# Even mixer of a two-layer hybrid network: latent products in two stream items, output projection from an earlier head, three transpose banks, float32 dilated groups

## The chip, the cores and the metric

One core of a Trainium2 chip runs the whole network in one launch. The metric is the device time of that launch in microseconds (us). Before the change the median of three runs is 1437.24 us (1437.18 to 1438.7).

## The reference, cut to what matters

512 tokens with 1024 features go through two layers; each adds a mixer and a gated feed-forward network (FFN) to the residual x. The change is almost wholly in the mixer of layer 0:

```python
def even_mixer(h, positions, w_in, q_norm, w_uq, kv_norm, w_ukv, w_out):
    proj = h @ w_in
    ...
    for gi, (window, dilation) in enumerate(DSW_GROUPS):      # (128,1), (512,4), (2048,16)
        og, lg = dilated_window_attention(q[:, :, sl], k[:, :, sl], v[:, :, sl], window, dilation)
    ...
    y_a = jnp.sum(wts[..., None] * jnp.stack(outs, axis=0), axis=0)   # 4 heads
    qm = (rmsnorm(c_q, q_norm) @ w_uq)                                # 12 latent heads
    kv = (rmsnorm(c_kv, kv_norm) @ w_ukv)
    ...
    y_b = causal_softmax_attention(q_full, k_full, v_m, (MLA_NOPE + MLA_ROPE) ** -0.5)
    return jnp.concatenate([y_a, y_b], axis=-1) @ w_out
```

The other mixer (a state-space scan, SSD, and stick-breaking attention), both FFNs and the norms are computed as before.

## The kernel before, in words

Activations lie with features on the 128 partitions and tokens along the free axis, so a tile is 128 x 512. Every large product keeps float32 accuracy by splitting both operands into a rounded part and a rest (hi and lo, type float32r) and doing three products: hi·hi, lo·hi, hi·lo (`mm3`, L113 is the one line that issues them). A weight chunk is loaded (`wraw`, SP queue), ACT copies it to `whi` (L220), and DVE, or POOL in the FFNs, subtracts to give `wlo` (L222). There are two buffers of each.

PE works strictly in the order in which the program was written (`InOrder`); the other engines' orders are set by a scheduler that replays the dependences. The even mixer is written as two interleaved sequences:

- A loop over 16 heads: twelve latent (MLA) heads in six pairs, and 2 x 2 dilated heads (each treats the three dilation groups g = 0, 1, 2 of one head). For each head: its scores (bank tag `s`), softmax (L580 to L584 on DVE and ACT), transposes of the probabilities (tag `t`), the copy to `pth`/`ptl` (hi on ACT, lo on DVE; L601/L602 in latent heads, L954/L955 in dilated ones), the products with the values (tag `o`), and `head_out` (L618 on ACT, L619 on DVE), which adds the two 64-partition halves of `o` into `yp`. The next head's scores stand between this head's value products.
- A `Stream` of items that fill PE between those steps, piece by piece (three products of 512 columns each, `st.fill`): the projections for the dilated heads (`d{p}{g}{s}`, tag `proj`), the latent products (`m{pr}`), the splitting of y (`y`) and the output projection (`o{m}`). `st.until(name)` drains the stream up to an item; `st.held` keeps an item back until a given head. `_load` fetches the chunk of the current item and of the one after it.

An item `m{pr}` (`run_mla`) does, all in `proj` banks: the value product (evicted by `vt`, L761), the key product (`knp`, L766), and two query products (`rt`, L775, split L265/L266); after the first of those the values are transposed and split (`token_split`, L629/L630). PSUM has eight banks of 512 columns: in this phase `proj`, `s`, `t` and `o` have two each. The output projection multiplies seven of the eight tiles of y in items `o0` to `o7`, released at head 14; the eighth tile (the second dilated pair's) follows in `run_tail`, eight outputs alternating between `s` and `proj`. `residual` (L367, DVE) adds each to x. Then `ffn` begins: its first two weight chunks, `norm` (`xh` on ACT, `xl` on DVE, L331/L332), the sum of squares.

In SSD, after the scores of 16 heads, `gate_norm(0)` (L1433) forms a row of 1/rms values by PE into a `t` bank, copied by ACT (`rsr`, L311); it stood at head 14, just ahead of two `gate` transposes, which use `t` as well.

Of the kernel before, what the change touches and what calls it, by code (L numbers as in the profile page):

```python
# [52 lines left out]
F_M, F_D0, F_D1 = (1, 1, 2), (2, 1.5, 3), (2, 2, 4)  # L53
# [65 lines left out]
class Stream:  # L119
# [12 lines left out]
    def _load(self, i):  # L132
        if i < len(self.items) and i not in self.loaded:
            self.loaded[i] = self.items[i][1]()

    def step(self, upto=None):

        while True:
            if self.gen is None:
# [3 lines left out]
                self._load(self.at + 1)  # L143
# [41 lines left out]
class Builder:  # L185
# [169 lines left out]
    def run_tail(self, src, kt, y, banks=("proj",)):  # L355

        def run(w):
            for m in range(KT):
                ps = self.psum(banks[m % len(banks)])
                self.gemm(ps, w, m * P, P, 0, {kt: y[kt][0]}, {kt: y[kt][1]}, [kt])  # L360
                self.residual(m, ps)
                yield

        return f"t{kt}", lambda: self.wchunk(src, D), run

# [4 lines left out]
    def build(self):  # L370
# [29 lines left out]
        with self.phase("l0", s=2, t=2, o=2) as pool:  # L400
            self.even_mixer(pool)
# [219 lines left out]
    def token_split(self, pool, src, tag, bufs):  # L621
# [5 lines left out]
        pv = pt.rearrange("p (b h d) -> p b h d", b=NB, h=2)  # L627
        v = pool.tile([P, NB, 2, 2, 64], F32R, tag=tag, name=self.nm(tag), bufs=bufs)
# [16 lines left out]
    def even_mixer(self, pool):  # L645
# [109 lines left out]

        def run_mla(pr):
            def run(w):
                vps = self.psum("proj")
                self.gemm(vps, w, 640, P, 0, klh, kll, [0])
                vt = pool.tile([P, T], F32, tag="tmp", name=self.nm("vt"), bufs=TMP)  # L760
                nc.vector.tensor_tensor(vt, vps, kr, op=ALU.mult)  # L761
                yield
                kps = self.psum("proj")
                self.gemm(kps, w, 512, P, 0, klh, kll, [0])
                knp = pool.tile([P, T], F32, tag="knp", name=self.nm("knp"), bufs=1)
                nc.vector.tensor_tensor(knp, kps, kr, op=ALU.mult)  # L766
                yield
                qs = []
                for e in range(2):
                    qps = self.psum("proj")  # L770
                    for i in range(2):
                        self.gemm(qps, w, e * P + i * 256, P, 256, qlh, qll, [i], i == 0, i == 1)
                        yield
                    t = pool.tile([P, T], F32, tag="tmp", name=self.nm("rt"), bufs=TMP)
                    nc.vector.tensor_tensor(t, qps, qt[e], op=ALU.mult)  # L775
                    qs.append(self.split(t, pool, **QK))
                    if e == 0:
                        v = self.token_split(pool, vt, "v", 3)
                yp = pool.tile([P, T], F32, tag="yp", name=self.nm("yp"), bufs=6)
                mla[pr] = qs, v, yp, knp  # L780

            return f"m{pr}", lambda: self.wchunk(a["wm0"][pr], 768), run

        def run_out(m):
            def run(w):
                yh, yl = {k: y[k][0] for k in range(7)}, {k: y[k][1] for k in range(7)}
                for ps in self.proj_pieces(w, yh, yl, range(7)):
# [3 lines left out]
            return f"o{m}", lambda: self.wchunk(a["wo0"][m], 896), run  # L791

        def run_y():
            def run(w):
                for i in range(6):
# [7 lines left out]
        def y_split(kt, yp):  # L803
# [7 lines left out]
               for p in range(2)]  # L811
        m = [run_mla(pr) for pr in range(6)]
        st = Stream(dsw[0][:3] + m[:1] + dsw[0][3:4] + m[1:2] + dsw[0][4:6] + m[2:3] + dsw[0][6:]
                    + dsw[1][:2] + m[3:4] + dsw[1][2:4] + m[4:5] + dsw[1][4:6] + m[5:] + dsw[1][6:]
# [921 lines left out]
```

## Time and profile before

| | |
|---|---|
| runs, median of three | 1437.24 us |
| profiled execution, own time | 1438.86 us |
| its span, first to last instruction | 1437.1 us |
| busy: PE, DVE, ACT, POOL | 96%, 59%, 47%, 32% |
| chain that ended last: PE, DVE, ACT, DMA | 80%, 11%, 5%, 1% |

The even mixer fills the first 340 us or so, its FFN follows to about 700, then SSD and stick-breaking attention to about 1020, the output projection of that mixer and the second FFN. A busy PE is not a PE at its peak: a product of 512 columns is shown as about 0.4 us long, but the next one starts 0.23 us later. So lost time must be looked for as idle time before instructions and as a lower granted clock (PEclk, 1.00 is full), not as a share of busy time.

### The profile page before, as it was taken

Reading aid. Unit: us, or ns where it says so; the run is one execution under the profiler, and the core shown is the slowest. Engines: PE = TensorE matmul, PEld = TensorE weight load, DVE = VectorE, ACT = ScalarE, POOL = GpSimd, SP = SyncE. Lnnn points to the kernel's source line nnn. Section 1 sums busy time; section 2 is a strip of 40 time slices with the busy share of each in tenths; the row PEclk is TensorE's granted clock in tenths of the full one; section 3 lists DMA queues with packets and bytes.
Section 4 is the critical chain, followed back from the end, with each engine's and each line's share of the span. In section 5 each row is a group of like instructions: output and inputs, shape, how many; then the busy total and the mean of one; then the engine's idle time right before and its main releaser. Section 6 shows DMA issues by size and latency. Waiting matters only on the chain.

```text
span 1437.1 us, 17873 instructions
## 1 busy us (share of the span) xinstructions
PE 1383.2 (96%) x6788; PEld 1141.8 (79%) x6788; DVE 845.6 (59%) x1313; ACT 681.7 (47%) x1119; POOL 454.7 (32%) x297
## 2 busy tenths in 40 slices
PE   7898989899999999999999998999999999999997
PEld 5687777787888888888878887787888888888886
DVE  7978678756555555221478775889555555552124
ACT  5478658744433333222355555787344333332222
POOL 2100000002655555444302620222025555554441
PEclk9999999999999999999999999999999999999999
DMA  4322112122232332333222111111233232333333
GB/s 166 112 70 63 56 55 72 40 67 88 88 103 88 103 94 97 94 94 98 88 88 89 59 60 46 59 45 48 77 96 96 95 103 89 102 99 90 101 95 99
DMA packets 40261, 121.19 MB, mean 84 GB/s; under 512 B 5232, under 2 KB 8304, under 8 KB 40176
## 3 DMA queue, kind: packets, MB, share of 16 engines
q1 hardware_dynamic: 38160, 117.92, 26.3%
q10 hardware_dynamic: 2016, 2.14, 0.5%
q8 instruction: 53, 0.87, 0.3%
q14 instruction: 32, 0.26, 0.1%
HBM read 114.80 MB, written 2.10 MB: 81 GB/s over the span
## 4 chain that ended last, share of the span: by engine, by line
PE 80%; DVE 11%; ACT 5%; issue 3%; DMA 1%; POOL 0%; SPq 0%; DVEq 0%; ACTq 0%; POOLq 0%
PE proj L113 50%; PE o L113 19%; PE z L113 5%; PE s L113 2%; PE t L116 2%; PE t L113 2%; DVE wlo L222 2%; DVE cv L1153 1%; ACT whi L220 1%; ACT s L582 1%; DVE xl L332 0%; DVE ptl L602 0%; ACT s L584 0%; DMA x<-in_x 0%; DVE x L367 0%
## 5 line engine op out<-in xcount | busy, mean ns | idle before, releaser
L222 POOL TENSOR_TENSOR wlo<-wraw,whi 128x1024 fp32r<-128x1024 f32 (+1 forms) x135 | 315.2, 2336 | 579.4 <-ACT whi L220 576.1
L220 ACT ACTIVATE whi<-wraw 128x1024 fp32r<-128x1024 f32 (+3 forms) x219 | 222.0, 1015 | 362.0 <-PE proj L113 324.7
L113 PE MATMUL proj<-xh,whi 128*128 128x512 f32 x844 | 343.6, 407 | 8.7 <-ACT xh L331 6.6
L113 PE MATMUL proj<-xh,wlo 128*128 128x512 f32 x844 | 334.2, 396 | 1.3 <-DVE wlo L388 1.1
L113 PE MATMUL proj<-xl,whi 128*128 128x512 f32 x844 | 334.3, 396 | 0.7 <-DVE xl L332 0.7
L113 PE MATMUL proj<-act,whi 128*128 128x512 f32 (+1 forms) x748 | 219.3, 377 | 0.0
L113 PEld LDWEIGHTS proj<-xh,whi 128*128 128x128 f32 x844 | 161.0, 191 | 42.1 <-ACT xh L331 9.3
L113 PEld LDWEIGHTS proj<-xh,wlo 128*128 128x128 f32 x844 | 160.9, 191 | 37.4 <-DVE wlo L388 1.5
L113 PEld LDWEIGHTS proj<-xl,whi 128*128 128x128 f32 x844 | 161.1, 191 | 30.8 <-DVE xl L332 2.4
L113 PEld LDWEIGHTS proj<-act,whi 128*128 128x128 f32 x748 | 137.6, 188 | 25.7
L113 PE MATMUL o<-xh,wlo 128*128 128x512 f32 x368 | 143.4, 390 | 0.0
L113 PE MATMUL o<-xh,whi 128*128 128x512 f32 x368 | 143.4, 390 | 0.0
L113 PE MATMUL o<-xl,whi 128*128 128x512 f32 x368 | 143.2, 389 | 0.0
L113 PE MATMUL proj<-act,wlo 128*128 128x512 f32 (+1 forms) x374 | 140.8, 376 | 0.0
L367 DVE TENSOR_TENSOR x<-x,proj 128x512 f32<-128x512 f32 x31 | 21.2, 684 | 171.3 <-PE proj L113 171.3
L525 DVE SCALAR_TENSOR_TENSOR cv<-gt,cols,cv 128x511 f32<-128x511 f32 x44 | 94.3, 2148 | 35.9 <-ACT cv L524 35.9
L222 DVE TENSOR_TENSOR wlo<-wraw,whi 128x1024 fp32r<-128x1024 f32 (+3 forms) x84 | 95.9, 1141 | 30.6 <-ACT whi L220 29.9
L528 ACT ACTIVATE sl<-cv 128x512 f32<-128x512 f32 x44 | 27.8, 631 | 127.3 <-DVE cv L526 127.3
L529 POOL TENSOR_TENSOR sl<-sl,rsr 128x512 f32<-128x512 f32 x44 | 57.8, 1313 | 94.3 <-ACT sl L528 94.3
L534 DVE TENSOR_TENSOR up<-sl,o 128x512 f32<-128x512 f32 x44 | 30.2, 687 | 91.8 <-POOL sl L529 91.8
L113 PEld LDWEIGHTS proj<-act,wlo 128*128 128x128 f32 x374 | 70.4, 188 | 12.9
L113 PEld LDWEIGHTS o<-xh,whi 128*128 128x128 f32 x368 | 69.2, 188 | 14.3
(301 smaller groups left out, 2106.4 us busy)
## 6 DMA issues: line engine op xcount, KB each, us to landing
wraw<-in_g SPq DMA_DIRECT2D x44, 512.0 KB, 3.3
wraw<-in_u SPq DMA_DIRECT2D x44, 512.0 KB, 3.3
wraw<-in_d SPq DMA_DIRECT2D x32, 448.0 KB, 3.3
wraw<-in_wqk SPq DMA_DIRECT2D x20, 512.0 KB, 3.6
wraw<-in_d SPq DMA_DIRECT2D x17, 512.0 KB, 3.6
wraw<-in_wx SPq DMA_DIRECT2D x12, 512.0 KB, 3.3
wraw<-in_wv SPq DMA_DIRECT2D x10, 512.0 KB, 3.9
wraw<-in_wz SPq DMA_DIRECT2D x8, 512.0 KB, 3.4
```

Source lines behind the costliest of these rows:

```text
L113: return self._put(self.b.nc.tensor.matmul(*args, **kw))
L116: return self._put(self.b.nc.tensor.transpose(*args))
L220: nc.scalar.activation(hi[:, :n], raw[:, :n], AF.Copy)
L222: (eng or self.lo).tensor_tensor(lo[:, :n], raw[:, :n], hi[:, :n].bitcast(F32), op=ALU.subtract)
L367: self.nc.vector.tensor_tensor(self.x[m], self.x[m], ps, op=ALU.add)
L525: nc.vector.scalar_tensor_tensor(c[:, 1:], gt[:, : T - 1], col_(1), c[:, 1:], op0=ALU.mult, op1=ALU.add)
L528: nc.scalar.activation(s, c, AF.Silu)
L529: nc.gpsimd.tensor_tensor(s, s, r, op=ALU.mult)
L534: nc.vector.tensor_tensor(u, s, pu, op=ALU.mult)
L582: nc.scalar.activation(t, t, AF.Exp, bias=nmx, scale=-1.0, accum_out=l)
L1153: nc.vector.scalar_tensor_tensor(c[:, d:], gt[:, : T - d], col_(j), c[:, d:], op0=ALU.mult, op1=ALU.add)
```

## The change

1. **Latent products in two items.** `m{pr}` now does value, key and first query product, `n{pr}` the second query product and the transposes of the values. Value and key products go to the two `s` banks; the first query product (in `proj`) is started between them. Pair 3 loads its chunk in two parts. The stream's order and the heads that release its items change with it, four pieces of the stream move from behind the first head's scores to ahead of them, and the stacking of the dilated queries and keys is placed earlier.
2. **Output projection sooner.** Six tiles of y (the latent pairs 0 to 4 and the first dilated pair) are multiplied in `o0` to `o7`, released at head 12 instead of 14. The latent pair 5 and the second dilated pair follow in `tail`, whose eight outputs lie in all of `s`, `t`, `o` and `proj`.
3. **Banks.** `t` has three, `o` one.
4. **Float32 dilated groups.** For g = 1 and 2 values and probabilities are copied once, in float32, without the DVE subtraction; one float32 product with 64 weight columns replaces two float32r products with 128.
5. **Loads further on.** `_load` passes over items that load nothing, so the next real chunk is fetched.
6. The first two chunks of each FFN get their `wlo` on DVE instead of POOL; SSD's `gate_norm(0)` moves from head 14 to head 13.

```diff
-F_M, F_D0, F_D1 = (1, 1, 2), (2, 1.5, 3), (2, 2, 4)
+F_M, F_D0, F_D1 = (1, 1, 2), (2, 1.5, 3), (2, 1, 2)
...
-                self._load(self.at + 1)
+                ahead = self.at + 1
+                while self._load(ahead) is None and ahead < len(self.items):
+                    ahead += 1
...
-        with self.phase("l0", s=2, t=2, o=2) as pool:
+        with self.phase("l0", s=2, t=3, o=1) as pool:
...
-        pre = [self.wchunk(w[0], D) for w in (wg, wu)]
+        pre = [self.wchunk(w[0], D, nc.vector) for w in (wg, wu)]
...
-    def token_split(self, pool, src, tag, bufs):
+    def token_split(self, pool, src, tag, bufs, split=True):
...
+        if not split:
+            v = pool.tile([P, NB, 2, 64], F32, tag=tag, name=self.nm(tag), bufs=bufs)
+            nc.scalar.activation(v, pv, AF.Copy)
+            return v
...
             def run(w):
-                vps = self.psum("proj")
-                self.gemm(vps, w, 640, P, 0, klh, kll, [0])
+                yp = pool.tile([P, T], F32, tag="yp", name=self.nm("yp"), bufs=6)
+                vps = self.psum("s")
+                self.gemm(vps, w, 384, P, 0, klh, kll, [0])
...
+                def keys():
+                    kps = self.psum("s")
+                    self.gemm(kps, w, 256, P, 0, klh, kll, [0])
...
+                yield from mla_query(pr, 0, w, keys)
...
+        def run_mla2(pr):
...
+                first = mla[pr].pop()
+                yield from mla_query(pr, 1, w or first, between, 0 if w else 512)
...
-                yh, yl = {k: y[k][0] for k in range(7)}, {k: y[k][1] for k in range(7)}
+                kts = (0, 1, 2, 3, 4, 6)
+                yh, yl = {k: y[k][0] for k in kts}, {k: y[k][1] for k in kts}
...
+        def tail():
+
+            banks = ("s", "t", "s", "t", "t", "o", "proj", "proj")
...
+            first = [(5, m) for m in range(4)]
+            rest = [p for m in range(4) for p in ((7, m), (5, m + 4))] + [(7, m) for m in range(4, 8)]
...
-        holds = {"d022": 5, "m3": 7, "d110": 7, "d122": 13, "y": 14}
+        holds = {"d022": 4, "m3": 5, "n3": 7, "d122": 11, "y": 12}
...
+                    if not split:
+                        hl.append(pool.tile([P, T], F32, tag="pth", name=self.nm("pth"), bufs=2))
+                        nc.scalar.activation(hl[0][:, :n], pt[:, :n], AF.Copy)
+                        return
...
         heads[0].prepare()
+        st.fill(4)
         for i in (3, 2, 1, 0):
             st.fill(1)
             heads[0].score(i)
-        st.fill(4)
+        st.fill(1)
...
-                          (14, gate_norm, 0), (14, gate, 1, 0), (14, gate, 1, 1), (15, gate, 1, 2)):
+                          (13, gate_norm, 0), (14, gate, 1, 0), (14, gate, 1, 1), (15, gate, 1, 2)):
```

Three places show how instructions move. The first is PE during the second head, where the latent products of pair 1 stand (`lh`/`ll` is the normed latent, `kh`/`kl` with `qk` are scores). Before, value and key product and a score between them:

```order
L113 MATMUL proj_746<-lh_365,whi_644 128x512
L113 MATMUL proj_746<-ll_366,whi_644 128x512
L113 MATMUL proj_746<-lh_365,wlo_646 128x512
L113 MATMUL s_752<-kh_572,qk_635 128x512
L113 MATMUL s_752<-kl_573,qk_635 128x512
L113 MATMUL s_752<-kh_572,qk_636 128x512
L113 MATMUL proj_762<-lh_365,whi_644 128x512
L113 MATMUL proj_762<-ll_366,whi_644 128x512
L113 MATMUL proj_762<-lh_365,wlo_646 128x512
```

Now, from the first half of the query product on; the value product, in an `s` bank too, stands eight rows ahead of it:

```order
L113 MATMUL proj_773<-lh_357,whi_644 128x512
L113 MATMUL proj_773<-ll_358,whi_644 128x512
L113 MATMUL proj_773<-lh_357,wlo_646 128x512
L113 MATMUL s_777<-kh_572,qk_638 128x384
L113 MATMUL s_777<-kl_573,qk_638 128x384
L113 MATMUL s_777<-kh_572,qk_639 128x384
L113 MATMUL s_787<-lh_365,whi_644 128x512
L113 MATMUL s_787<-ll_366,whi_644 128x512
L113 MATMUL s_787<-lh_365,wlo_646 128x512
```

The key product has gone from a `proj` bank to an `s` bank, behind a score that uses the other one. The second place is DVE at the same point, around the eviction `vt` of the value product. Before:

```order
L583 RECIPROCAL st_695<-st_695 128x1
L222 TENSOR_TENSOR wlo_744<-wraw_740,whi_742 128x1024
L761 TENSOR_TENSOR vt_750<-proj_746,rsr_519 128x512
L732 TENSOR_TENSOR rot_731<-proj_648,cos 128x512
L602 TENSOR_TENSOR ptl_719<-t_716,pth_718 128x128
```

Now (with the line numbers of the changed kernel):

```order
L572 ISA st_733 128x1
L772 TENSOR_TENSOR vt_761<-s_757,rsr_519 128x512
L225 TENSOR_TENSOR wlo_754<-wraw_750,whi_752 128x1024
L729 TENSOR_TENSOR rot_741<-proj_648,cos 128x512
L575 RECIPROCAL st_733<-st_733 128x1
```

The subtraction of the next weight chunk stands behind the eviction now, no longer ahead of it. The third place is PE in SSD, around the row of `gate_norm(0)` (`rsy` is its input, `xs` that of the `gate` transposes). Before:

```order
L113 MATMUL proj_7379<-xh_5902,whi_7273 128x512
L113 MATMUL proj_7379<-xl_5903,whi_7273 128x512
L113 MATMUL proj_7379<-xh_5902,wlo_7275 128x512
L113 MATMUL t_7428<-ident,rsy_7348 128x128 x4
L116 MATMUL t_7439<-ident,xs_5997 128x128 x4
L116 MATMUL t_7447<-ident,xs_5997 128x128 x4
```

Now (with the line numbers of the changed kernel):

```order
L113 MATMUL proj_7339<-xh_5846,whi_7233 128x512
L113 MATMUL proj_7339<-xl_5847,whi_7233 128x512
L113 MATMUL proj_7339<-xh_5846,wlo_7235 128x512
L113 MATMUL t_7357<-ident,rsy_7308 128x128 x4
L113 LDWEIGHTS idb
L113 MATMUL s_7368<-cm,idb 128x512
```

The two `xs` transposes follow the row only after twelve more projection products and a head's products, 20 rows on; the order has them directly behind it before.

More of the change, by code (lines that the diff above doesn't have):

```diff
@@ L754, in run_v, with mla_query @@
             return f"d{p}{g}2", lambda: self.wchunk(a["wv0"][g * 2 + p], D), run
+        def mla_query(pr, k, w, between, c0=0):
+            qps = self.psum("proj")
+            for i in range(2):
+                self.gemm(qps, w, c0 + i * P, P, P, qlh, qll, [i], i == 0, i == 1)
+                yield
+                if i == 0:
+                    yield from between()
+            t = pool.tile([P, T], F32, tag="tmp", name=self.nm("rt"), bufs=TMP)
+            nc.vector.tensor_tensor(t, qps, qt[k], op=ALU.mult)
+            mla[pr][0].append(self.split(t, pool, **QK))
         def run_mla(pr):
             def run(w):
-                vps = self.psum("proj")
-                self.gemm(vps, w, 640, P, 0, klh, kll, [0])
+                yp = pool.tile([P, T], F32, tag="yp", name=self.nm("yp"), bufs=6)
+                vps = self.psum("s")
+                self.gemm(vps, w, 384, P, 0, klh, kll, [0])
                 vt = pool.tile([P, T], F32, tag="tmp", name=self.nm("vt"), bufs=TMP)
@@ L762, in run @@
                 yield
[L763 to L778, printed above, removed]
@@ L779, in run @@
[L779 to L782 removed]
+                mla[pr] = [[], vt, yp, None, w]
+                def keys():
+                    kps = self.psum("s")
+                    self.gemm(kps, w, 256, P, 0, klh, kll, [0])
+                    knp = pool.tile([P, T], F32, tag="knp", name=self.nm("knp"), bufs=1)
+                    nc.vector.tensor_tensor(knp, kps, kr, op=ALU.mult)
+                    mla[pr][3] = knp
+                    yield
@@ new lines, in tail, with product, run, pieces @@
+        def tail():
+            banks = ("s", "t", "s", "t", "t", "o", "proj", "proj")
+            ps, ws = {}, []
+            def product(kt, m):
+                if kt == 5:
+                    ps[m] = self.psum(banks[m])
+                self.gemm(ps[m], ws[kt == 7], m * P, P, 0, {kt: y[kt][0]}, {kt: y[kt][1]}, [kt], kt == 5, kt == 7)
+                if kt == 7:
+                    self.residual(m, ps[m])
+            def run(which):
+                def pieces(w):
+                    ws.append(w)
+                    for p in which:
+                        product(*p)
+                        yield
+                return pieces
+            first = [(5, m) for m in range(4)]
+            rest = [p for m in range(4) for p in ((7, m), (5, m + 4))] + [(7, m) for m in range(4, 8)]
+            return [(f"t{i}", lambda i=i: self.wchunk(a["wo0b"][i], D), run(p)) for i, p in enumerate((first, rest))]
@@ L793, in run_y @@
         def run_y():
             def run(w):
-                for i in range(6):
+                for i in range(5):
                     y_split(i, mla[i][2])
@@ L867, in mla_head @@
             hd.fill_s, hd.fill_u, hd.fill_g = F_M
+            hd.needs = f"n{pr}"
             def prepare():
@@ L941, in score, with steps @@
                 probs[i] = self.softmax(pool, s, n, *(("s4", 5) if i else ("s3", 3)), mask)
-            def steps(o, blocks, uses):
+            def steps(o, blocks, uses, split=True):
                 hl = []
@@ L959, in apply @@
                     for v, cut, out, first, last in uses:
-                        for k in range(2):
-                            self.pe.matmul(out, v(), cut(hl[k]), start=first and k == 0, stop=last and k == 1,
+                        for k in range(len(hl)):
+                            self.pe.matmul(out, v(), cut(hl[k]), start=first and k == 0, stop=last,
                                            skip_group_check=True)
@@ L1017, in even_mixer @@
             heads[0].score(i)
-        st.fill(4)
+        st.fill(1)
         for k, hd in enumerate(heads):
             nxt = heads[k + 1] if k + 1 < len(heads) else None
+            st.held -= {name for name in holds if holds[name] <= k}
+            if hd.needs:
+                st.until(hd.needs)
+            if k == 8:
+                values(3)
             units = hd.units()
             n = len(units)
-            st.held -= {name for name in holds if holds[name] <= k}
+            if k in (4, 11):
+                stack(k // 11, 0)
             if nxt:
@@ L1049, in even_mixer @@
                 st.fill(hd.fill_g)
-        st.add([self.run_tail(a["wo0b"], 7, y, ("s", "proj"))])
+        st.add(tail())
         st.finish()
```

59 lines of the change are left out of this document (35 added, 24 removed).

## The prediction

> **What bounds the kernel now.** I read the page first, then the busy time by stage, then PE's own waits, then the granted clock around them. The page's head and PE row:
>
> ```profile
> span 1437.1 us, 17873 instructions
> PE 1383.2 (96%) x6788; PEld 1141.8 (79%) x6788; DVE 845.6 (59%) x1313; ACT 681.7 (47%) x1119; POOL 454.7 (32%) x297
> ```
>
> The busy time by stage (PE, weight load, DVE, ACT, POOL, then clock, DMA share, GB/s) shows two kinds of stage:
>
> ```profile
> 60.00:80.00 20.00, 15.19 (x60) 11.04 (x59) 15.01 (x30) 11.87 (x24) 0.00 (x0) 0.91 0.22 66
> 80.00:140.00 60.00, 54.94 (x291) 45.34 (x290) 52.43 (x123) 48.31 (x109) 0.00 (x0) 1.00 0.23 66
> 140.00:200.00 60.00, 54.74 (x386) 44.56 (x385) 36.91 (x74) 35.03 (x68) 0.00 (x0) 0.94 0.17 50
> 200.00:280.00 80.00, 73.77 (x445) 60.35 (x444) 67.85 (x156) 63.18 (x139) 0.00 (x0) 1.00 0.23 66
> 346.00:700.00 354.00, 353.76 (x1573) 293.00 (x1572) 154.93 (x146) 121.57 (x151) 183.06 (x89) 1.00 0.31 95
> 860.00:1020.00 160.00, 150.70 (x767) 125.12 (x766) 125.17 (x227) 106.62 (x184) 26.05 (x49) 0.98 0.16 49
> ```
>
> In the first FFN (346 to 700) PE never stops: 354 us / 1573 products = 0.225 us for a product of 512 columns, which is the pace used below. Nothing in the change shortens that. In the even mixer PE loses time, and DVE is close behind it: 52.43/60 = 87% busy from 80 to 140, 67.85/80 = 85% from 200 to 280. So the gain is at most what PE waits for there, and DVE caps it. PE's waits from 60 to 346 us (total, times, longest):
>
> ```profile
> PE proj L113 <- DVE vt L761: 7.4, 6, 2.0
> PE o L113 <- DVE ptl L602: 4.7, 5, 1.2
> PE s L113 <- DVE qk L266: 3.2, 2, 2.8
> PE t L116 <- DVE ptl L955: 2.7, 1, 2.7
> PE t L116 <- DVE v L630: 2.4, 3, 1.1
> PE proj L113 <- DVE x L367: 1.6, 1, 1.6
> PE o L113 <- ACT pth L601: 0.9, 2, 0.5
> PE proj L113 <- DVE xl L332: 0.7, 1, 0.7
> PE s L113 <- ACT qk L265: 0.5, 1, 0.5
> PE proj L113 <- DVE rot L732: 0.4, 1, 0.4
> ```
>
> They add up to 24.5 us. No row waits for a DMA, so the loads further on are worth nothing by themselves. The rows of `vt`, `ptl` L955 and `v` are waits for a bank, not for data. In SSD, from 860 to 880, one more stands:
>
> ```profile
> PE t L116 <- ACT rsr L311: 2.6, 1, 2.6
> ```
>
> Four stretches of waiting cost twice, since the clock halves right behind them. The first and third row here (PE busy 0.79 and 0.82 of 3.3 us) are two of the waits, the row behind each shows the clock at 0.50; the last two rows are the other such stretches, at the first scores and in the fourth head:
>
> ```profile
> 181.80:185.10 3.30, 0.79 (x6) 0.42 (x4) 3.23 (x5) 2.34 (x4) 0.00 (x0) 1.00 0.00 0
> 185.20:188.50 3.30, 3.25 (x10) 2.77 (x11) 1.28 (x2) 0.60 (x1) 0.00 (x0) 0.50 0.42 159
> 867.90:871.20 3.30, 0.82 (x6) 0.81 (x7) 2.72 (x4) 3.20 (x6) 0.00 (x0) 1.00 0.12 31
> 871.30:874.60 3.30, 3.30 (x13) 2.81 (x13) 3.24 (x6) 0.87 (x2) 0.00 (x0) 0.50 0.31 123
> 72.60:75.90 3.30, 3.30 (x10) 2.72 (x10) 1.45 (x6) 2.00 (x4) 0.00 (x0) 0.50 0.41 149
> 140.80:144.10 3.30, 3.30 (x11) 2.74 (x10) 1.38 (x2) 1.47 (x3) 0.00 (x0) 0.50 0.03 13
> ```
>
> A stretch of some 3.3 us at half speed costs half of it, 1.7 us.
>
> **The change part by part.** Minus is a gain. The number of 512-column products stays the same, so what counts is waiting.
>
> *Latent products.* The value eviction was late because DVE stood in the next chunk's subtraction:
>
> ```profile
> 81.06 1.22 DVE L222 TENSOR_TENSOR wlo<-wraw,whi 128x1024 fp32r<-128x1024 f32 x1 [2.22 <-ACT whi L220]
> 82.20 0.68 DVE L761 TENSOR_TENSOR vt<-proj,rsr 128x512 f32<-128x512 f32 x1
> 82.94 0.49 PE L113 MATMUL proj<-lh,whi 128*128 128x512 f32 x1 [1.05 <-DVE vt L761]
> 83.27 0.39 PE L113 MATMUL proj<-ll,whi 128*128 128x512 f32 x1
> ```
>
> Now `vt` stands ahead of that subtraction, and the query product has a `proj` bank of its own. But value and key products take `s` banks, and by the order an `s` bank is then used again after only 6 to 9 products (1.4 to 2.0 us) at some ten places more. The six `vt` waits average 7.4/6 = 1.2 us; 1.14 of it (82.20 - 81.06) was the subtraction. That leaves next to nothing; since DVE is 87% busy I take 0.2 us at each of the ten, 2.0 in all. Of 7.4 + 0.4 (`rot`, the same bank) the gain is **-5.8** (bounds -7.8, nothing left, and 0, the same waits on `s`).
>
> *Third `t` bank.* In the order the shortest distance between a `t` tile's last transpose and the next use of its bank grows from 1.45 us of products to 2.5. The waits of 2.7 and 2.4 go: **-5.1** (bounds -5.1 and, if half stays, -2.5).
>
> *`gate_norm(0)` at head 13.* In SSD the second `gate` transpose waited 2.6 us for the copy out of a `t` bank; 20 PE rows now lie between. The row's own input is ready only just then, for which I leave 0.3: **-2.3** (bounds -2.6 and 0). Next in line on DVE are the four norm products, ahead of the last head's `mh`; by the order PE has two pieces and a head's products more before it needs that.
>
> *First scores.* Two more pieces, 6 products, stand ahead of the first score: 6 x 0.225 = **-1.35** of the 3.7 (3.2 + 0.5). The rest stays, since the split that it waits for is the same twelfth DVE instruction behind `vt`:
>
> ```profile
> 71.34 1.28 DVE L266 TENSOR_TENSOR qk<-rt,qk 128x512 fp32r<-128x512 f32 x2
> ```
>
> Bounds -3.7 and 0.
>
> *Value products.* Waits for `ptl` and `pth` are 5.6. In the order, places where 2.2 us of PE work or less lie between a head's transposes and the products that use them fall from six to three. All three are in the last head, where the stream has run dry (before, 17 pieces were left behind it): once 1.0 us of cover against the 2 or so that copy, subtraction and the way between need. I take -4.0 and +1.5: **-2.5** (bounds -5.6 and +1.5).
>
> *Float32 groups.* Eight float32r products of 128 columns took 173.30 - 172.35 = 0.95 us, so the pair that is replaced costs 0.24. The nearest float32 product has 64 columns and 128 weight columns; eight records (two for each product) took 854.91 - 854.11 = 0.80, 0.20 each:
>
> ```profile
> 172.35 0.33 PE L113 MATMUL o<-pth,v 128*128 128x128 f32 x1
> 173.30 0.39 PE L113 MATMUL s<-qk,qk 128*128 128x128 f32 x2
> 854.11 1.00 PE L113 MATMUL o<-xdt,mh 128*128 128x64 f32 x8
> 854.91 0.48 PE L113 MATMUL proj<-xh,whi 128*128 128x512 f32 x1
> ```
>
> For 32 products the range is 32 x (0.20 - 0.24) = -1.2 to, if twice the columns cost twice as much, 32 x (0.40 - 0.24) = +5.1. The weight columns halve while the moving ones double, so I take **0**. DVE sheds 8 of the `ptl` and 4 of the `v` rows, 12 x 0.69 = 8.3 us:
>
> ```profile
> L955 DVE TENSOR_TENSOR ptl<-t,pth x16: 539/688/693, 163.6 to 311.4; 128x512 fp32r<-128x512 f32 x12, 128x384 fp32r<-128x384 f32 x4
> L630 DVE TENSOR_TENSOR v<-t,v x12: 670/691/708, 69.3 to 281.9; 128x512 fp32r<-128x512 f32 x12
> ```
>
> *One `o` bank.* The next head's first value product must now wait for `head_out`. A typical and the longest case, last product and DVE sum:
>
> ```profile
> 103.17 0.39 PE L113 MATMUL o<-ptl,v 128*128 128x512 f32 x1
> 104.76 0.69 DVE L619 TENSOR_TENSOR yp<-o,yp 64x512 f32<-64x512 f32 x1
> 116.12 0.39 PE L113 MATMUL o<-ptl,v 128*128 128x512 f32 x1
> 121.12 0.66 DVE L619 TENSOR_TENSOR yp<-o,yp 64x512 f32<-64x512 f32 x1
> ```
>
> From end to end: 105.45 - 103.56 = 1.9 and 121.78 - 116.51 = 5.3 us. By the order 3.7 us of PE work lie between two latent heads, so 1.9 is hidden and 5.3 costs 1.6. I take one full case and some small ones: **+2.0** (bounds 0 and +19, below). [...]
>
> *Restarts.* Behind a wait the next product starts 83.27 - 82.94 = 0.33 us later instead of 0.225. Some 15 waits fewer: 15 x 0.1 = **-1.5**.
>
> *Clock.* The stretches behind 181.8 and 867.9 go with their waits, the one at 72.6 probably stays, the one at 140.8 is open: two of four, 2 x 1.7 = **-3.4** (bounds -6.8 and +1.7, one new).
>
> *End of the mixer.* Before, PE waited 1.6 (`x`) and 0.7 (`xl`). Now 12 pieces of `tail` stand there and y's last split has 15 products, 3.4 us, of cover for four short steps; the FFN's first gate needs a `proj` bank that `x` tile 6 holds, and on DVE two subtractions of 1.2 us (as the row at 81.06), formerly POOL's, stand between the residuals. **+1.0** (bounds -2 and +4). Pair 3's chunk in two loads adds one short load on SP and one copy and subtraction; nothing waits on that queue.
>
> *DVE as the cap.* From 80 to 140 DVE's 52.4 us must fit into what is left of 60. Taking all the waits there out would leave it above 95%: **+2.0** given back.
>
> Sum: -5.8 - 5.1 - 2.3 - 1.35 - 2.5 + 0 + 2.0 - 1.5 - 3.4 + 1.0 + 2.0 = -17.0. The profiled execution's own time, 1438.86 us (span 1437.1 and 1.8 around it), becomes 1421.9. It lies 1.6 above the median of the runs, 1437.24, which becomes **1420**.
>
> **The rivals.**
>
> *DVE takes the place of PE's waits.* For it: 87% and 85% busy, and `s` banks that are emptied by DVE alone. Against it: 8.3 us less work there, and eight pieces of products moved from the end into the heads. Then only the `t` banks, the SSD wait and its clock are gained: -5.1 - 2.3 - 1.7 + 1 = -8, **1429**.
>
> *The single `o` bank binds: slower.* If `head_out` came as late as in the longest row at each of the 12 changes behind a latent head, 12 x 1.6 = +19.2 in place of the +2.0: -17.0 - 2.0 + 19.2 = +0.2; with two new half-speed stretches, +3.6, **1441**. It decides from a mean of 3.7 + 19/12 = 5.3 us on. Against it: the typical 1.9.
>
> *The half-speed stretches do not hang on these waits.* The rows show them behind 2.5 us of idleness in 3.3; that is four cases. If they came anyway, the sum loses 3.4: **1423.6**. [...]
>
> *It doesn't move the time.* The pieces moved out of the end are missing in the last head, and what is gained before is lost there; that needs 17 us of waits in one head and the `tail`, more than all bank waits of the stage together: **1437**.
>
> **How the numbers follow.** Forecast 0.61. Alone it reaches from 1413 (value products at -5.6, a third stretch of the clock gone, no wait on `o`: 6.8 lower) to 1427 (latent products at -3, `o` at +4, the end at +3: 6.8 higher). DVE 0.20, clock 0.10, `o` bank 0.06, no change 0.03. The range takes in the first three: below, the forecast's end and nothing left of the waits on `s` (2.0), above, the DVE case and an end of the mixer 2 us worse: **1411 to 1431**. A measurement of this kernel can tell 0.2%, 2.9 us, from no change. Faster 0.90, same 0.04, slower 0.06.
>
> **What would show it.** Right: PE's `vt`, `v` and dilated `ptl` waits gone or under 2 us; no `rsr` wait in SSD; half-speed stretches fewer; DVE over 88% from 80 on. Wrong: rows in which PE's `o` products wait for DVE's `yp`, or `s` products for `vt`, `knp` or the softmax, of more than 5 us in total; a wait for `x` above 4 us at the start of the FFN; float32 products at 0.4 us each.

## The result, and the profile after

The median is 1429.89 us (five runs, 1427.74 to 1431.39) against 1437.24 us (five runs, 1433.94 to 1438.7): a ratio of 0.995 with an interval of 0.9933 to 0.9966. In a second series the ratio was 0.9943 (0.993 to 0.9956). So it is faster, as forecast, but by 7.4 us (8.9 in the second series) instead of 17: about half. The profiled execution took 1429.99 us, its span was 1428.3.

The page's head, and the busy time by stage (PE, weight load, DVE, ACT, POOL, clock, DMA share, GB/s):

```profile
span 1428.3 us, 17887 instructions
PE 1383.2 (97%) x6788; PEld 1139.2 (80%) x6788; DVE 838.0 (59%) x1307; ACT 680.4 (48%) x1121; POOL 445.6 (31%) x293
```

```profile
60.00:80.00 20.00, 16.74 (x70) 12.75 (x69) 15.73 (x32) 12.18 (x26) 0.00 (x0) 0.91 0.20 59
80.00:140.00 60.00, 53.85 (x275) 44.09 (x274) 48.51 (x114) 44.99 (x102) 0.00 (x0) 0.97 0.21 62
140.00:200.00 60.00, 58.19 (x407) 46.32 (x405) 40.24 (x80) 36.40 (x71) 0.00 (x0) 1.00 0.24 70
200.00:280.00 80.00, 77.03 (x426) 64.48 (x429) 64.40 (x149) 62.10 (x137) 0.00 (x0) 0.98 0.20 63
```

PE is busier from 140 to 280 (135.2 us, before 128.5). From 80 to 140, the stage in which DVE was fullest, it is not (53.85, before 54.94), and the clock there is now 0.97. DVE fell to 81% there; the forecast had it rise above 88%. PE's waits from 60 to 340 us:

```profile
PE o L113 <- DVE ptl L594: 3.7, 5, 1.5
PE t L116 <- ACT s L576: 2.9, 3, 1.2
PE s L113 <- DVE qk L269: 2.8, 1, 2.8
PE o L113 <- DVE yp L611: 2.6, 3, 1.1
PE o L113 <- ACT xh L334: 1.6, 1, 1.6
PE o L113 <- DVE ptl L1014: 1.2, 1, 1.2
PE s L113 <- DVE xl L854: 0.7, 1, 0.7
PE o L113 <- ACT pth L593: 0.6, 1, 0.6
```

With four smaller rows they add up to 17.8 us, before 24.5. The rows for `vt` and the `t` banks are gone. In their place stand a wait for data, the probabilities (`s`, scaled by ACT as the last step of the softmax), and a wait for a bank, the emptying of the one `o` bank (`yp`). The `ptl` and `pth` rows have stayed (5.5, before 5.6). What such a new wait looks like, on PE and then on DVE:

```profile
92.86 0.30 PE L113 MATMUL o<-pth,v 128*128 128x128 f32 x1 [1.10 <-DVE yp L611]
93.56 0.33 PE L113 MATMUL o<-ptl,v 128*128 128x128 f32 x1 [0.41 <-DVE ptl L594]
...
90.34 0.93 DVE L225 TENSOR_TENSOR wlo<-wraw,whi 128x768 fp32r<-128x768 f32 x1
91.31 0.69 DVE L923 TENSOR_TENSOR kl<-knp,kh 64x512 fp32r<-64x512 f32 x1
92.03 0.68 DVE L611 TENSOR_TENSOR yp<-o,yp 64x512 f32<-64x512 f32 x1
92.63 0.67 DVE L269 TENSOR_TENSOR qk<-rt,qk 128x512 fp32r<-128x512 f32 x1
93.23 0.28 DVE L594 TENSOR_TENSOR ptl<-t,pth 128x128 fp32r<-128x128 f32 x1
```

ACT had done its half of `yp` at 89.53 (its row at 88.94 takes 0.59 us); DVE came to the other half at 92.03, behind a subtraction of the next weight chunk and a key split.

Where the time came from, by the same instruction in both traces: the sum of squares of the first FFN starts at 346.9 us (before 350.8), the last `xdt` product of SSD at 866.6 (874.5), the first product `z` of the stick-breaking attention at 882.2 (890.2). So 3.9 us come from the even mixer and 4.0 from the end of SSD: the sums of squares for its gate still start 3.9 us sooner (852.5, before 856.4), so the FFN and most of SSD between add nothing. Another 1.4 come before the output projection of that mixer, which starts at 1012.6 (1022.0), where a half-speed stretch at 905 is not there any more (clock 1.00 from 850 to 1020, before 0.98); 0.6 are lost again in the last 10 us, where PE falls to half speed sooner before the end (at 1420.4 of 1428.3, before at 1431.0 of 1437.1).

### The profile page after: what moved, and what is told of

Same layout as the page of the kernel before. It is cut to its first block, busy times and chain, and to the rows that moved or that the text cites. A ratio compares the mean times of both kernels' runs of the same rounds, so it can differ in the third digit from the quotient of the medians.

```text
span 1428.3 us, 17887 instructions
## 1 busy us (share of the span) xinstructions
PE 1383.2 (97%) x6788; PEld 1139.2 (80%) x6788; DVE 838.0 (59%) x1307; ACT 680.4 (48%) x1121; POOL 445.6 (31%) x293
## 4 chain that ended last, share of the span: by engine, by line
PE 81%; DVE 11%; ACT 4%; issue 2%; DMA 1%; POOL 0%; SPq 0%; DVEq 0%; ACTq 0%; POOLq 0%
PE proj L113 50%; PE o L113 20%; PE z L113 5%; PE s L113 3%; PE t L113 2%; PE t L116 2%; DVE wlo L225 1%; DVE cv L1219 1%; ACT whi L223 1%; DVE s L572 0%; DMA x<-in_x 0%; ACT s L574 0%; DVE ab L1635 0%; DVE xl L335 0%; ACT yp L610 0%
## 5 line engine op out<-in xcount | busy, mean ns | idle before, releaser
L225 POOL TENSOR_TENSOR wlo<-wraw,whi 128x1024 fp32r<-128x1024 f32 (+1 forms) x131 | 305.8, 2335 | 585.5 <-ACT whi L223 525.8
L113 PE MATMUL proj<-xh,wlo 128*128 128x512 f32 x836 | 330.0, 395 | 1.3 <-DVE wlo L380 1.1
L113 PE MATMUL proj<-xl,whi 128*128 128x512 f32 x836 | 330.2, 395 | 1.0 <-DVE xl L335 1.0
L113 PEld LDWEIGHTS proj<-act,whi 128*128 128x128 f32 x748 | 137.6, 188 | 25.9
L113 PE MATMUL proj<-act,wlo 128*128 128x512 f32 (+1 forms) x374 | 140.8, 376 | 0.0
L225 DVE TENSOR_TENSOR wlo<-wraw,whi 128x1024 fp32r<-128x1024 f32 (+4 forms) x90 | 101.1, 1123 | 30.9 <-ACT whi L223 30.5
L113 PEld LDWEIGHTS o<-xl,whi 128*128 128x128 f32 x370 | 69.6, 188 | 14.5
```

Of the source, the lines that this page charges most:

```text
L113: return self._put(self.b.nc.tensor.matmul(*args, **kw))
L225: (eng or self.lo).tensor_tensor(lo[:, :n], raw[:, :n], hi[:, :n].bitcast(F32), op=ALU.subtract)
```

## The experiments

Each kernel was timed beside the kernel before. Since what is lost to half-speed stretches varies from run to run (8.6 to 15.8 us over 23 runs of the kernel before, shown below), two numbers stand beside the ratio: the time *net of the clock*, span times granted clock, as the mean of all timed runs, given as a difference to the kernel before in the same series; and the rest, which is *lost to the clock*. A clock is read to 0.001, 1.4 us in one run; the standard error of the means is 0.1 to 0.6 us (1.2 for wlo on POOL).

| kernel | median us | ratio (interval) | net us | lost us |
|---|---|---|---|---|
| before, by series | 1436.2 to 1438.2 | 1 | 0 | 11.6 to 12.6 |
| changed, second series | 1429.26 | 0.9943 (0.993 to 0.9956) | -7.1 | 10.7 |
| before + gate_norm at 13 | 1431.41 | 0.997 (0.9957 to 0.9982) | -1.8 | 8.9 |
| before + banks | 1433.63 | 0.9986 (0.9973 to 0.9999) | -2.5 | 12.1 |
| before + `s` for value and key | 1435.98 | 1.0 (0.9987 to 1.0014) | -3.1 | 15.0 |
| before + 4 pieces first | 1438.26 | 1.0014 (1.0002 to 1.0025) | +2.7 | 10.8 |
| before without wlo | 1423.2 | 0.9922 (0.9904 to 0.994) | -11.9 | 11.9 |
| changed without wlo | 1410.88 | 0.9826 (0.9808 to 0.9844) | -19.1 | 5.3 |
| changed, old banks | 1427.59 | 0.9928 (0.9915 to 0.9942) | -6.6 | 9.4 |
| changed, float32r groups | 1430.08 | 0.994 (0.9928 to 0.9953) | -6.7 | 10.9 |
| changed, old stacking | 1428.41 | 0.9936 (0.9923 to 0.9948) | -7.4 | 10.8 |
| changed, wlo in halves | 1428.68 | 0.9944 (0.9929 to 0.9959) | -7.4 | 11.4 |
| changed, wlo on POOL | 1431.32 | 0.9952 (0.994 to 0.9965) | -3.9 | 9.7 |
| changed, wlo on POOL in the heads | 1423.09 | 0.9907 (0.9892 to 0.9922) | -9.2 | 8.0 |
| changed, output projection later | 1424.76 | 0.9921 (0.9906 to 0.9937) | -8.0 | 8.0 |
| changed + 4 pieces first | 1421.6 | 0.9893 (0.9874 to 0.9912) | -11.7 | 8.5 |
| that + POOL in the heads | 1421.55 | 0.9901 (0.9884 to 0.9919) | -11.1 | 8.2 |
| that + projection later, no POOL | 1422.46 | 0.9897 (0.9883 to 0.9912) | -12.5 | 9.1 |

### Parts of the change alone, on the kernel before

```diff
-                          (14, gate_norm, 0), (14, gate, 1, 0), (14, gate, 1, 1), (15, gate, 1, 2)):
+                          (13, gate_norm, 0), (14, gate, 1, 0), (14, gate, 1, 1), (15, gate, 1, 2)):
```

> The kernel before, with gate_norm(0) at head 13 and nothing else changed. Forecast's step: the 2.6 us wait for rsr goes, 0.3 is left, and the half-speed stretch behind it (1.7 us) goes with it: -4.0 us, the clock at 1.00 from 865 to 880. Rival (half-speed stretches do not hang on such a wait): -2.3, with a stretch at 0.5 elsewhere within some 20 us.

The wait for `rsr` is gone, the clock is 1.00 at 871 (before 0.50), and 1.8 us net are gained beside 2.3 forecast; the ratio stands for 4.3 us (2.6 to 6.2), since less went to the clock as well (8.9 us, beside 11.8 in the runs of before). The forecast's step holds.

```diff
-        with self.phase("l0", s=2, t=2, o=2) as pool:
+        with self.phase("l0", s=2, t=3, o=1) as pool:
```

> The kernel before, with three t banks and one o bank and nothing else changed. Forecast's steps: -5.1 for the t waits, +2.0 for the o bank, and a half-speed stretch less (-1.7): -4.8. Theory of the queues (what DVE and ACT hand on late is waited for at the next place that needs it): the t waits come back as waits of o products for yp, ptl or pth, in total no more than 1 us gained.

PE's waits there, 60 to 340 us:

```profile
PE proj L113 <- DVE vt L761: 8.5, 6, 2.1
PE o L113 <- DVE ptl L602: 4.1, 4, 1.2
...
PE o L113 <- DVE yp L619: 1.7, 2, 1.0
...
PE t L116 <- ACT s L584: 1.1, 1, 1.1
```

The 5.1 us of waits for `t` banks are gone, as forecast; 1.7 for `yp` and 1.1 for the probabilities are new, and `vt` has grown by 1.1. The rows gain 1.8 in all, the clock-free time 2.5: between the two theories, and about half of what the rows of before said.

```diff
-                vps = self.psum("proj")
+                vps = self.psum("s")
...
-                kps = self.psum("proj")
+                kps = self.psum("s")
```

> The kernel before, with value and key products in s banks instead of proj banks and nothing else changed (the items and their order stay). Forecast's step: -5.8 us, the waits of proj products for vt (7.4) gone. Theory of the queues: those waits go, and the scores' s banks then wait for vt and knp, or the softmax comes later: less than half, -3 us at most.

3.1 us net, and nothing in the median, since 3.4 us more went to the clock than in the runs of before. PE's rows fall by only 0.8 (24.5 to 23.7), and some of the 3.1 lies in the way of counting: the five runs that lost least to the clock (11.5 to 12.9 us) have a net time of 1420.9 us on average, the seven others 1419.1. By the five alone the move is worth 2.1. The waits moved: `vt` is still waited for, now by `s` and `t`, and the dilated `ptl` wait grew from 2.7 to 4.1:

```profile
PE t L116 <- DVE ptl L955: 4.1, 1, 4.1
...
PE s L113 <- DVE vt L761: 2.7, 3, 1.1
...
PE t L116 <- DVE vt L761: 0.8, 2, 0.6
```

The three parts alone are worth 1.8 + 2.5 + 3.1 = 7.4 us net; the whole change is worth 7.1. If they simply added, everything else in it would come to about nothing; that they add is not shown, and the next run speaks against it for the banks.

### Parts of the change undone

```diff
-        with self.phase("l0", s=2, t=3, o=1) as pool:
+        with self.phase("l0", s=2, t=2, o=2) as pool:
...
-            banks = ("s", "t", "s", "t", "t", "o", "proj", "proj")
+            banks = ("s", "t", "s", "t", "o", "o", "proj", "proj")
```

> The changed kernel, with two t and two o banks as before. Forecast's price: the yp waits (2.6 us) go and t waits of up to 5.1 us come back: +2.5 us. Theory of the queues: a bank only says where the late copy is waited for, so within 1.5 us of the changed kernel.

```profile
PE t L116 <- DVE v L627: 3.6, 3, 1.6
PE o L113 <- DVE ptl L594: 3.1, 3, 1.8
...
PE o L113 <- ACT pth L593: 2.1, 1, 2.1
PE t L116 <- DVE ptl L594: 1.9, 1, 1.9
PE t L116 <- ACT v L623: 1.0, 1, 1.0
```

The rows changed names: the `yp` and softmax waits are gone, 6.5 us of waits for `t` banks are back (19.6 us in all), and the net time is the same to 0.5 us. In the changed kernel these two arrangements of the banks only decide where a late copy is waited for.

```diff
-                    uses = [(val(g, r_), lambda t, r_=r_: cut(t, r_), cut(o, r_)[0:64], False, g == 2 and r_ == 3)
+                    uses = [(val(g, r_), lambda t, r_=r_: cut(t, r_), cut(o, r_), False, g == 2 and r_ == 3)
...
-                    out.append(steps(o, blocks, uses, False))
+                    out.append(steps(o, blocks, uses))
...
-                vs[p, g] = self.token_split(pool, raws[p, g, 2], "v", 3, g == 0)
+                vs[p, g] = self.token_split(pool, raws[p, g, 2], "v", 3)
```

> The changed kernel, with the dilated groups g = 1, 2 in two float32r products again: 8.3 us more on DVE, and by the trace 32 products of 0.22 us in place of 0.255 (-1.2 us on PE). Theory of the queues: the waits for ptl and yp near 140 to 205 and 280 to 320 grow by more than the 1.2: +1 to +4 us. Rival (DVE's work there is off the path): -1.2 us.

Within 0.5 us net: PE's waits grow by 2 us (`ptl` L1014 from 1.2 to 1.8, `rt` by 0.6, and smaller ones), and the products are cheaper by 1.2. The price of the float32 products is in the trace of the changed kernel, where the eight records of four products start at 200.11 and the next instruction at 201.13:

```profile
200.11 1.09 PE L113 MATMUL o<-pth,v 128*64 128x128 f32 x8
201.13 0.66 PE L116 MATMUL t<-ident,vt 128*128 128x128 f32 x4
```

That is 1.02 us for four, 0.255 each. All eight groups took 8 x 1.02 = 8.2 us; the pairs they replace took 0.95 + 0.99 + 6 x 0.84 = 7.0. So +1.2 us, inside the forecast's bounds and not at its 0.

```diff
-        holds = {"d022": 4, "m3": 5, "n3": 7, "d122": 11, "y": 12}
+        holds = {"d022": 4, "m3": 5, "n3": 7, "d122": 12, "y": 13}
```

> The changed kernel, with d122 and the output projection held one head longer (12 and 13 instead of 11 and 12), so that the stream has nothing for ten of its places in heads 11 and 12. Forecast's step (products of the output projection as cover for copies and subtractions): waits for ptl and pth in heads 11 and 12 come back, +2 to +4 us. Rival (DVE is late there, cover or not): within 1 us, waits of the same total as now.

It is 0.9 us net faster than the changed kernel, not 2 to 4 slower, and its waits add up to 17.8 us as in the changed kernel: `ptl` and `yp` grew by 0.5 and 0.9, and the last head's wait (`ptl` L1014, 1.2) and the one for `xl` (0.7) went. In heads 11 and 12 themselves, where ten places are empty, the waits for the probabilities and their copies are 1.0 us beside 0.45. So the products of the output projection as cover there are worth about 0.5 us and not 2 to 4; the end of the mixer gained more from them.

```diff
+                    stack(p, 0)
                     stack(p, 1)
...
-            if k in (4, 11):
-                stack(k // 11, 0)
```

> The changed kernel, with the stacking of the dilated queries (4 ACT copies and 2 more, 2 DVE subtractions) back in the preparation of the dilated heads instead of one or two heads earlier. If the earlier stacking is what makes PE wait for the softmax at 115 and 116 us (1.7) and for pth and ptl behind it (2.1) and at 223 (2.1): those go and the time falls by 2 to 5 us. Theory of the queues without a special part for the stacking: they come back one head later, within 1.5 us of the changed kernel.

The rows of PE's waits are those of the changed kernel to 0.1 us, and so is the time: the scheduler puts ACT's copies at the same places (the same order around them), so this run says nothing on the question. It serves as one more run of the changed kernel.

### DVE's work

```diff
+        if self.no_lo:
+            return hi, hi
         lo = self.wp.tile([P, 1024], F32R, tag="wlo", name=self.nm("wlo"))
...
+            self.no_lo = True
             self.even_mixer(pool)
+        self.no_lo = False
```

> The kernel before, with the subtraction that gives wlo left out in the even mixer (whi stands in its place; the product count stays): 36.8 us less work on DVE there. Theory of the queues: PE's 24.5 us of waits from 60 to 346 fall by half or more: -12 us or better. Rival (the waits are too little PE work between a step and its use, whatever else DVE does): the six vt waits go (1.1 us each was the subtraction, -6.8) and the rest stays: -7 us, the ptl waits still at 4 us or more.

> The changed kernel, with the subtraction that gives wlo left out in the even mixer (whi stands in its place; the product count stays): 39.5 us less work on DVE there. Theory of the queues: PE's 17.8 us of waits from 60 to 340 fall to 8 or less: -9 us or better, yp and ptl first. Rival (too little PE work between): -3 us or less, ptl, yp and softmax waits within 30% of what they are now.

Before without wlo, and the changed kernel without it:

```profile
PE s L113 <- DVE qk L268: 2.7, 1, 2.7
PE proj L113 <- DVE vt L765: 2.2, 3, 1.5
PE t L116 <- DVE ptl L959: 1.9, 1, 1.9
PE t L116 <- DVE v L634: 1.9, 3, 1.0
```

```profile
PE t L116 <- ACT s L580: 1.9, 3, 1.5
PE o L113 <- DVE x L361: 1.6, 1, 1.6
PE o L113 <- DVE ptl L598: 1.6, 2, 1.0
PE o L113 <- ACT pth L597: 1.3, 1, 1.3
```

The waits fall by 9.9 us (24.5 to 14.6) and by 9.8 (17.8 to 8.0), the net time by 11.9 and by 12.0. DVE's weight subtractions, 36.8 and 39.5 us from 40 to 345 (12 and 13% of that time), therefore cost PE some 12 us in either kernel, though DVE is idle for an eighth of the time or more in every stage of both.

Without them the change is worth 19.1 - 11.9 = 7.2 us, as much as with them. But that equal sum hides two opposite shifts. In the kernel before, the subtraction was itself most of what the latent products waited for: their rows (`vt`, `rot`, `rt`) are 7.8 with it and 2.8 without, so the change has less to remove there. Everything else gains: apart from these rows PE's waits go from 16.7 to 17.0 through the change when DVE does the subtractions, and from 11.8 to 8.0 when it does not. The wait for `yp` (2.6) is gone, that for the probabilities is 2.1 instead of 2.9, that for the first scores 0.3 instead of 2.8. So DVE's load did eat some 4 us of the waits that the rest of the change would have taken away.

```diff
-        (eng or self.lo).tensor_tensor(lo[:, :n], raw[:, :n], hi[:, :n].bitcast(F32), op=ALU.subtract)
+        for c in ((slice(0, n // 2), slice(n // 2, n)) if self.halves else (slice(0, n),)):
+            (eng or self.lo).tensor_tensor(lo[:, c], raw[:, c], hi[:, c].bitcast(F32), op=ALU.subtract)
```

> The changed kernel, with each wlo subtraction of the even mixer in two halves of about 0.65 us on DVE. If it is the place of a 1.2 us instruction ahead of an urgent one that costs (order), waits for yp, ptl and vt fall by a third: -2 to -4 us. If it is DVE's whole load (volume, some 30 x 0.1 us more), nothing or +1.

0.3 us net: `yp` and the softmax fell by 1.4 together, `ptl` and `pth` rose by 1.2. A shorter instruction ahead of an urgent one is not enough.

```diff
-        self.lo = nc.vector
+        self.lo = nc.gpsimd
         with self.phase("l0", s=2, t=3, o=1) as pool:
```

> The changed kernel, with the wlo subtractions of the even mixer on POOL, which is idle there, instead of DVE; all work is still done. Theory of the queues: as with the subtractions left out, the waits for ptl, yp and the softmax fall, about -8 us beside the changed kernel. Rival (the queue that matters is then POOL's): wlo itself comes later, PE waits for it, and DVE's instructions get longer beside a busy POOL; -2 to +5 us, with rows of PE waiting for POOL wlo.

The start lost 8.7 us (the first score at 76.4 instead of 67.7; the granted clock of this execution was 0.989, beside 0.991 in that of the changed kernel), the heads gained 6.0. Kept to the heads:

```diff
+        self.lo = nc.gpsimd
         for k, hd in enumerate(heads):
```

> The changed kernel, with the wlo subtractions on POOL from the first head on only (the start of the kernel keeps them on DVE); all work is done. In the run that had them on POOL from the start, the stretch from the first scores to the next FFN's sum of squares took 273.2 us, 6.0 less than in the changed kernel, and the start lost 8.7. Theory of the queues: -6 us beside the changed kernel, waits for yp and ptl down by half. Rival (a POOL instruction of 2.2 us beside DVE slows DVE as much as it relieves it): within 1.5 us.

2.1 us net better than the changed kernel, and 2.7 less lost to the clock. `yp` fell from 2.6 to 0.4 and the softmax from 2.9 to 1.7, `ptl` did not, and POOL's own lateness is new:

```profile
PE o L113 <- DVE ptl L594: 3.7, 5, 1.7
...
PE s L113 <- POOL wlo L225: 1.2, 1, 1.2
...
PE o L113 <- DVE yp L611: 0.4, 1, 0.4
```

### Products ahead of the first score

```diff
-        st.fill(4)
+        st.fill(8)
         for i in (3, 2, 1, 0):
```

> The changed kernel, with four more pieces (12 products, 2.7 us) ahead of the first score. The wait there is 2.8 us and a half-speed stretch follows it in every profile so far: -2.7 and -1.7 if nothing else hangs on it, -4.4 us. Theory of the queues: the four pieces are missing as cover in the first heads; the wait is found again there, and only the clock's 1.7 is gained.

> The kernel before, with four pieces more ahead of the first score and nothing else changed. If cover at the start is worth as much there as in the changed kernel: -2.7 and the half-speed stretch behind it, -4.4 us; the forecast's step for the first scores is then right in size for its 6 products and stopped short of what was to be had. If the pieces are missing later (the stream of the kernel before runs dry in heads 4 and 6): -1 us or less.

In the changed kernel the wait for `qk` fell from 2.8 to 0.8 and the others did not come back (13.9 us in all, from 17.8): 4.6 us net, 1421.6 us. In the kernel before, four more pieces, put in as a line of their own, cost 2.7 us net (ratio 1.0014, 1.0002 to 1.0025): `qk` fell from 3.2 to 0.9, but `ptl` rose from 4.7 to 5.8, `rot` by 0.8, and 1.1 for the probabilities, 0.9 for a `t` bank and 0.8 for `knp` are new (25.9 us in all, from 24.5). This fits a stream that in the changed kernel has four pieces to spare and before has not; which later places lack them is not shown.

> The changed kernel with both edits that helped it: four more pieces ahead of the first score, and wlo on POOL from the first head on. Net of the half-speed clock they gained 5.3 and 2.8 us. If PE's cover at the start and DVE's queue in the heads are separate causes: -8 us net beside the changed kernel, about 1418. If both only gave DVE time for the same late steps: no more than the better of the two, about 1421.

> The changed kernel with four more pieces ahead of the first score and the output projection one head later. Net of the clock the two edits alone gained 5.3 and 1.2 us. If each stands for itself: 1.2 us net below the run with the four pieces. If they share the cause (DVE's and ACT's late steps): no gain beside that run, or a loss, since the stream then runs dry in head 11 by four pieces more.

Four pieces and POOL do not add up: 1421.55 us beside 1421.6, and net 11.1 below the kernel before where the sum of the single gains is 13.7. POOL brings nothing beside the four pieces. The later projection brings 0.8 of its 0.9 net (12.5; the sum is 12.6), which the median of five runs does not show (1422.46). The best that the experiments point to is the changed kernel with the four pieces, 15 us faster than before.

### The same kernel again

> The changed kernel itself, unaltered, in another series. If the half-speed stretches are set by where a wait falls in the clock's 3.4 us grid and not by the wait alone, PE's waits are the same to 0.2 us and the number of stretches varies from run to run: the time net of them (span times granted clock) 1416 to 1417 us, the loss to the clock 8 to 13 us. Rival (each wait brings its stretch): the loss is the same in each run to 1.5 us.

Every wait row is the same to 0.1 us. Over 11 runs of the changed kernel the net time is 1416.6 us and 8.6 to 12.9 are lost to the clock, 10.9 on average; over 23 runs of the kernel before it was 8.6 to 15.8, 11.8 on average. So the same waits cost up to 7 us more or less from run to run.

## Why the prediction was right in sign and wrong in size

Net of the clock the forecast was -13.6, and -7.1 was measured. Three rows nearly account for it: -6.7 (PE's waits, 24.5 to 17.8), -1.8 (`gate_norm`), +1.2 (float32) make -7.3.

**Latent products, -5.8.** The rows of its bank (`vt`, `rot`, now `rt`) fell by 7.0, and 0.4 came on `s`: right by the rows. As a cause it is smaller as far as was tried: the move to `s` banks, without the split into two items, is worth 2 to 3.

**Third `t` bank -5.1, one `o` bank +2.0.** Row by row both came (-5.1, +2.6). As causes they failed: alone the two give -2.5, and taking them back costs 0.5. "The waits of 2.7 and 2.4 go" was true, and the 5.1 us did not go with them.

**Value products, -2.5.** This is the step that failed by most: the waits for `ptl` and `pth` were 5.6 and became 5.5. It rested on counting PE's products between a head's transposes and their use, and left short places in the last head alone. But only 1.2 of the 5.5 lie there; 4.3 lie in heads where the count had found more than 2.2 us of PE work. For one of them, PE and then DVE:

```profile
122.27 0.33 PE L113 MATMUL o<-ptl,v 128*128 128x128 f32 x1 [1.47 <-DVE ptl L594]
...
119.81 1.22 DVE L225 TENSOR_TENSOR wlo<-wraw,whi 128x1024 fp32r<-128x1024 f32 x1
120.95 1.07 DVE L729 TENSOR_TENSOR rot<-proj,cos 128x512 f32<-128x512 f32 x1
121.93 0.62 DVE L594 TENSOR_TENSOR ptl<-t,pth 128x128 fp32r<-128x128 f32 x2
```

The transposes ended at 117.77. ACT had `pth` done at 120.42, itself behind three other copies, and DVE came to `ptl` at 121.93, behind a weight subtraction and a `rot`. The run with the output projection later takes the cover away in two heads and is no slower; the runs without wlo take load from DVE and halve the rows (5.6 to 2.5 before, 5.5 to 2.9 in the changed kernel). So these waits hang on when DVE and ACT come to the copies more than on PE's products between.

**DVE as the cap, +2.0.** Found as 2.9 us of waits for the probabilities, and by the runs without wlo worth some 4 us in all. The mechanism was not that of a full engine: DVE was at 81%, not above 95%, and still late. The forecast's sign for it (over 88%) was wrong.

**First scores, -1.35:** 3.7 to 2.8, -0.9. **Float32, 0:** +1.2. **`gate_norm`, -2.3:** -1.8. **End of the mixer, +1.0:** 2.3 to 2.8, +0.5. **Restarts, -1.5:** nothing is left for them in the account above; the term took 15 waits fewer, and PE's rows count 23 before and 20 after.

**Clock, -3.4.** -0.9 to -1.2 on average (11.8 to 10.9 over all runs, 11.9 to 10.7 in the second series). The two stretches that it named (181.8, 867.9) are gone with their waits; three others in the mixer came at new waits. It failed in taking one profiled execution's stretches for the kernel's.

Between 17.0 and the 8.3 of the second series (7.1 and 1.2) lie 8.7 us. All but 0.2 has a place: 3.1 are waits (9.75 forecast, 6.7 found; above all the value products), 2.2 the clock, 1.5 the restarts, 1.2 float32, 0.5 `gate_norm`.

The rival with DVE in the place of PE's waits gave 1429, the time that came, and its account was half right: DVE's load does take gains back, as the runs without wlo show, but it had the latent products gain nothing, and their rows fell by 7.0. That its time came out is partly luck. The rival on the clock was half right: the stretches do follow waits, but not each. The single `o` bank did not bind (2.6 us).

Of the signs of being right, only the one on DVE's load did not come, and of the signs of being wrong none did (`o` products wait 2.6 us for `yp`, `s` products 0.4 for the softmax). Each of these signs looks at one row; together they could not tell 7 us from 17.

What stays open: why, in detail, a wait taken away at a bank comes back at the probabilities; and why the four pieces and the relief of DVE do not add up. That both only give DVE's and ACT's late steps time is argued, not shown. No run takes the split into two items, the loads further on or the new places of the heads alone.

## What to carry to other kernels

Where an engine that copies for PE is late, the rows of waits name the place and not the cause: add up what the rows give only after asking what the same late engine delivers next; here about half came. Counting one engine's work between two steps does not say when another engine comes to the step between; look at what stands ahead of it in its own order. Test a new arrangement of banks by taking it back, and look for spare cover where one long wait stands at the start of a stage. Where two variants cost the same in sum, compare their rows before calling a cause cleared. Compare times net of the granted clock, over several runs, where effects are a few us.

## What the runs showed of the hardware

**The half-speed stretches lie on steps of 3.413 us.** In the profiled execution of the kernel before they start at 45.2, 72.5, 140.8, 185.1, 871.2 and 905.3, which is 0, 8.0, 28.0, 41.0, 242.0 and 252.0 steps of (905.3 - 45.2)/252 = 3.413 us. In that of the changed kernel they start at 44.8, 72.1, 123.3, 225.7 and 335.0: 0, 8.0, 23.0, 53.0 and 85.0 such steps. Cut into windows on these steps, the trace shows how busy PE was ahead of a stretch. Four windows of the changed kernel in a row:

```profile
113.20:116.60 3.40, 2.35 (x9) 1.37 (x8) 2.01 (x7) 3.32 (x8) 0.00 (x0) 1.00 0.00 0
116.60:120.00 3.40, 2.53 (x11) 1.78 (x11) 1.65 (x5) 3.30 (x7) 0.00 (x0) 1.00 0.03 7
120.00:123.35 3.35, 1.41 (x8) 1.18 (x9) 2.62 (x5) 2.78 (x9) 0.00 (x0) 1.00 0.24 61
123.40:126.70 3.30, 3.30 (x13) 2.91 (x12) 2.17 (x4) 0.35 (x1) 0.00 (x0) 0.50 0.62 179
```

Waits of 0.65 and 1.05 us split over two windows (busy 2.35 and 2.53) left the clock at 1.00; those of 0.62 and 1.47 us, mostly in one window (1.41 busy), were followed by 0.50. In these two executions, from 36 us to 1400 us, PE was busy for 0.57 to 1.68 us in eight of the windows of 3.41 us, and each of the eight was followed by one at half speed. Of all others, busy for 1.88 us or more, three were: the one at 901.9 of the kernel before (2.22 busy), and in each kernel the one told of next. So what these waits of some 2 us brought hung on how much of them fell into one window.

**A window filled by products of one column was followed by half speed.** In both executions the stretch at 45 us follows a window in which PE is shown as busy throughout (3.41 us). In the changed kernel:

```profile
41.83 2.73 PE L113 MATMUL t<-ones,sq 128*128 128x1 f32 x24
45.51 0.63 PE L113 MATMUL proj<-xh,whi 128*128 128x512 f32 x1
```

24 records of one column each take 2.7 us of its 3.4, and the products behind it take 0.63 us instead of 0.39. In the kernel before the same 24 take 2.7 us from 42.3 on, and the products behind them 0.63 us. No run puts other work in the place of these products, so it is not shown that they are the cause.

**Two `rot` on DVE took 2.4 us beside a subtraction on POOL.** With wlo on POOL in the heads, 2.2 us each on average and 2.4 in this row:

```profile
96.19 2.41 POOL L225 TENSOR_TENSOR wlo<-wraw,whi 128x1024 fp32r<-128x1024 f32 x1 [7.17 <-ACT whi L223]
...
96.28 0.69 DVE L772 TENSOR_TENSOR vt<-s,rsr 128x512 f32<-128x512 f32 x1
97.13 2.42 DVE L729 TENSOR_TENSOR rot<-raw,cos 128x512 f32<-128x512 f32 x1 [0.17 <-ACT raw L728]
```

`vt`, which reads a bank, takes 0.69 us beside POOL, as in the changed kernel. `rot`, which reads two SBUF tiles and takes 1.08 us in the changed kernel, takes 2.42 here and ends 0.95 us after POOL; so does the next one beside POOL (2.34 us, from 105.72 to 108.06, with POOL at work until 107.11). What held them is not shown.
